# A hybrid mixer and MLP block on one core: gates by one Tanh, decays made earlier, a norm row by a product, and one product moved forward

## The chip, the core and the metric

The kernel runs on 1 core of a Trainium2 chip. TensorE (PE) multiplies, VectorE (DVE), ScalarE (ACT) and GpSimd (POOL) work element by element, and SyncE (SP) issues the DMAs, one after the other. The metric is device time in microseconds (us) of one execution; less is better. Three runs of the kernel before gave 1247.94, 1253.7 and 1256.1 us, with a median of 1253.7 us.

## What is computed

A sequence of 16 meta tokens and 1024 tokens, 1024 channels wide, goes through one block. All is float32. Cut to what matters here:

```python
u = rmsnorm(h, norm_mix)                        # y * g: a row of 1024 factors
a, q, k, v, r, lr, ga, gb = split(u @ w_in)
y_a = (multiscale_pool(a) @ w_pool_mix * pool_scale) @ w_pool_out
log_a = log_sigmoid(lr @ w_gate_up + b_gate) / 16        # decays, 256 wide
o = gla_chunked(q / 8, k, v, log_a)             # gated linear attention, chunks of 64
o = rmsnorm(o, gla_norm) * silu(r)              # silu(r) = r * sigmoid(r)
y_b = o @ w_gla_out
m = sigmoid(ga) * y_a + sigmoid(gb) * y_b
h = h + m @ w_out
h = h + square(relu(rmsnorm(h) @ w_ff1)) @ w_ff2
out = rmsnorm(h)[16:]
```

## The kernel before, in words

Data lie transposed: channels on the 128 partitions, 1024 tokens as two halves of 512 columns. PE has no exact float32 path at full rate here, so each float32 operand is split into a high part (`w1h`, `th`) by an ACT copy and a low part (`w1l`, `tl`) by a DVE subtraction, and `mm3` (L256) multiplies three times: high by high (L260), low by high and high by low (L261, L262). A product of one 512-row slice by 512 columns is 4 times 3, or 12 matmuls.

The order of PE's instructions is written out by hand. The other engines' orders are made by a scheduler from the program and its own estimates, and each engine, SP too, goes through its list strictly in order: an instruction that waits holds all behind it.

The stages are these.

- **Opening** (`start`, L391). SP loads `x` tile by tile; each tile is normalized (`layer_norm`, L227: a square with a sum on ACT, small steps on DVE, and a DVE product L234 with the norm row `gB`, a copy of the 1024 factors on all partitions that a 512 KB broadcast DMA makes, L414), turned by PE (L246), copied out (L202, L203, L249) and multiplied by the columns of `v` and `lr` (`v_tile`, L350). `warm` (L407) gives PE work on a blank tile.
- **Plain stage.** Blocks of 128 columns of `w_in` for `a` (L483) and `k` (L520), 8 by 24 matmuls and more each, with the pooling (`mix_block`, L495) between. `W1` is a ring of two weight blocks: when a block is done, the next but one is loaded and split (L75, L76). Their results leave through three PSUM banks `mm`.
- **Pairs** (`pairs_of_projections`, L688). The 22 blocks of q, r, gb and ga go two at a time through seven products instead of eight: P1, P2, P5, P6, P7, P4, P3. The differences of `x` that they need are made by `differences` (L529), the sums of weights by POOL (`sums_weights`, L641), and each is split by ACT (L609) and DVE (L610). `pairs_order` (L633) sets the order. P2 adds to the PSUM bank in which P1 stands, and P1 must be copied to `u2p` (L720) before it. The first pair's weights start in `first_pair` (L676). The tile of differences `xr` lies where `fs` and `u2p` lie afterwards, so the last one, made by `last_difference` (L551, split at L541 and L542), must be over before POOL writes `fs`.
- **What leaves the pairs.** `sigmoid` (L563) is the log of the sigmoid: Abs, Exp and Ln on ACT (L566, L567, L568) and one step on DVE (L569). `put_gate` (L583) stores it for ga and gb, and the Exp that ends it comes later, by `open_gate` (L967, instruction L970). `put_r` (L577) takes it on with an Exp (L579) and a DVE product (L580).
- **Inside a chunk** (`inside`, L842), four times, spread between the pairs' products. The decays `g` come from `log_decay` (L776: one product L779 into bank `gs`, four ACT steps, one DVE step) and an Exp (L855). Then levels 0 to 5 double the blocks: DVE and ACT grow the tiles `n` and `f` (L873, L875, L874), PE makes scores (L834) from them, and DVE writes those under a mask (L902). `meta_state` (L797) does the same for the 16 meta tokens.
- **Merge** (`gla`, L1107, and what follows). The attention across chunks (L1044 to L1105) runs between the products for y_a (`ya_block`, L976) and y_b (`yb_block`, L1004); the gates come back from DRAM, are opened by L970 and multiplied in (L996, L1025), and the sum is split again (L1029, L1030). Then `w_out`, the second norm, and the two MLP layers, which the change does not touch.

Of the kernel before, what the change touches and what calls it, by code (L numbers as in the profile page):

```python
# [103 lines left out]
def kernel(  # L104
# [50 lines left out]
    q_dram = dp.tile([2, 2, P, HALF], F32, name="q_dram")  # L155
    pm_dram = dp.tile([4, 2, P, HALF], F32, name="pm_dram")
# [234 lines left out]
    def start():  # L391
# [20 lines left out]
        warm(6)  # L412
        nc.sync.dma_start(ident, ident_in)
        nc.sync.dma_start(gB, bcast(norm_mix))  # L414
        for t in range(8):
# [9 lines left out]
            if t == 0:  # L425
                nc.sync.dma_start(S["lrraw"], w_in[:, C_LR : C_LR + 16].rearrange("(k p) c -> p k c", p=P))
                ask_vw(0)
                load(1)
                load(2)
                warm(10, P)  # L430
                load_vw(0)
                ask_vw(1)
# [29 lines left out]
    def quad(a):  # L462
        return a.rearrange("p (k c) -> p k c", k=4)

# [91 lines left out]
    for f, i in ((a_, 0), (a_, 1), (m_, 0), (a_, 2), (m_, 1), (a_, 3), (m_, 2), (k_, 0), (m_, 3)):  # L556
        f(i)
# [3 lines left out]
    step(one, lambda: S["last_difference"]())  # L561

    def sigmoid(b):  # L563

        t = nxt("t1")
        act.activation(t, b, ACT.Abs)  # L566
        act.activation(t, t, ACT.Exp, scale=-1.0)  # L567
        act.activation(t, t, ACT.Ln, bias=1.0)  # L568
        dve.scalar_tensor_tensor(t, b, 0.0, t, ALU.min, ALU.subtract)  # L569
# [7 lines left out]
    def put_r(h, half, b, o):  # L577
        t, o = sigmoid(b), o or nxt("c")
        act.activation(t, t, ACT.Exp)  # L579
        dve.scalar_tensor_tensor(o, b, gnorm[:, h : h + 1], t, ALU.mult, ALU.mult)  # L580
        nc.sync.dma_start(r_dram[h, half], o)

    def put_gate(dram):  # L583
        return lambda d, half, b, o: nc.sync.dma_start(dram[d, half], sigmoid(b))
# [48 lines left out]
    def pairs_order(n_pairs):  # L633
        yield from (("P1", 0), ("P2", 0), ("P5", 0))
        for i in range(1, n_pairs + 1):
            for p in ("P6", "P1", "P7", "P5", "P4", "P2", "P3"):
                n = i if p in ("P1", "P5", "P2") else i - 1
                if n < n_pairs:
                    yield p, n

    def sums_weights(order, n_pairs, load, eng):  # L641
# [5 lines left out]
        for p, i in order(n_pairs):  # L647
# [3 lines left out]
            else:  # L651
                a21, a22 = (w1raw[i, 1][:, k : k + 4] for k in (0, 4))
                s = quad(S["fs"][:, i % 2] if p != "P7" else S["s3"])
# [34 lines left out]
    def pairs_of_projections():  # L688
# [18 lines left out]
        for n, (p, i, (ah, al)) in enumerate(ahead(pair_weights(), 3)):  # L707
# [17 lines left out]
            elif p == "P7":  # L725
# [3 lines left out]
                put(d + 1, 1, c, c)  # L729
            elif p == "P4":  # L730
# [20 lines left out]
            if total - n == 3:  # L751
                raw.back()
                W1.shift = 1
                enqueue(rest)
                W1.top_up(1)
            yield

# [18 lines left out]
    def log_decay(lrT, p, n, dst, y, t):  # L776

        b = two("gs")[:, 0, :n]
        pe.matmul(b, wgu[:, p * P : (p + 1) * P], lrT, start=True, stop=True)  # L779
        act.activation(y, b, ACT.Identity, bias=bgate[:, p : p + 1])  # L780
# [755 lines left out]
```

## Time and profile before

The profiled execution took 1249.28 us, of which the program's span is 1247.4 us; 1.9 us lie around it.

| stretch of the span (us) | what runs | PE busy | DVE busy | ACT busy | DMA share |
|---|---|---|---|---|---|
| 0 to 26 | opening, up to the third tile | 22.16 | 15.31 | 18.00 | 0.83 |
| 26 to 152.6 | rest of the opening, plain stage | 126.39 | 64.62 | 56.57 | 0.28 |
| 152.6 to 408 | pairs, with the work inside chunks | 245.92 | 191.93 | 166.81 | 0.43 |
| 408 to 525 | across chunks, merge | 110.93 | 82.80 | 53.54 | 0.81 |
| 525 to 628 | `w_out`, second norm | 102.25 | 60.48 | 40.97 | 0.31 |
| 628 to 1247.4 | MLP, last norm | 605.99 | 450.91 | 299.45 | 0.50 |

How to read it: PE is busy nearly always, so what another engine does costs time only where PE waits for it. A row of the profile gives in brackets how long an engine stood idle before an instruction and which instruction ended that idle time. PE's matmuls overlap: a row's length is not the step from one to the next, which is read from their starts.

### The profile page before, as it was taken

The numbers are of one execution on the slowest core, as the hardware profiler recorded it, in microseconds if no ns is written. First come the engines' busy times: TensorE is split into PE (matmuls) and PEld (weight loads), VectorE is DVE, ScalarE is ACT, GpSimd is POOL, SyncE is SP. The second block draws the span as 40 slices with busy tenths as digits, with TensorE's granted clock in tenths as the row PEclk, the third lists the DMA queues.
The fourth block names the chain that finished last, engine by engine and source line by source line (L and its number), as shares of the span: only waits on it lengthen the run. The fifth ranks groups of instructions, "written<-read, shape, count | busy, mean of one in ns | idle before, by whom it ended". The sixth has DMA issues, their size and how long they took to land.

```text
span 1247.4 us, 18416 instructions
## 1 busy us (share of the span) xinstructions
PE 1213.6 (97%) x6807; PEld 997.3 (80%) x6807; DVE 866.0 (69%) x1421; ACT 635.3 (51%) x1119; POOL 72.2 (6%) x95
## 2 busy tenths in 40 slices
PE   8999999999999999999999999999999999999997
PEld 6999877777777778788778888888878788888776
DVE  5635548796877478844897676676664887887686
ACT  7623456767576434523655454554554444445454
POOL 0000042322321000000000000000000000000000
PEclk9999999999999999999999999999999999999999
DMA  8212342434347976941245444444579763333532
GB/s 259 81 39 85 94 127 76 136 97 141 80 134 229 327 264 200 311 138 51 101 125 161 145 157 150 157 152 144 168 241 368 274 214 102 102 93 93 169 91 86
DMA packets 153401, 192.23 MB, mean 154 GB/s; under 512 B 12096, under 2 KB 89168, under 8 KB 153312
## 3 DMA queue, kind: packets, MB, share of 16 engines
q1 hardware_dynamic: 153312, 191.06, 47.6%
q8 instruction: 53, 0.87, 0.3%
q14 instruction: 36, 0.29, 0.1%
HBM read 129.14 MB, written 61.88 MB: 153 GB/s over the span
## 4 chain that ended last, share of the span: by engine, by line
PE 76%; DVE 9%; DMA 8%; ACT 4%; issue 3%; SPq 1%; POOL 0%; DVEq 0%; ACTq 0%; POOLq 0%
PE b_o L261 7%; PE b_o L262 7%; PE b_o L260 7%; PE b_mm L262 6%; PE b_mm L260 6%; PE b_mm L261 6%; PE b_y L260 5%; PE b_y L261 5%; PE b_y L262 5%; PE b_sc L260 3%; PE b_sc L261 3%; PE b_z L260 3%; PE b_sc L262 3%; PE b_z L261 3%; PE b_z L262 3%
## 5 line engine op out<-in xcount | busy, mean ns | idle before, releaser
L609 ACT ACTIVATE w1h<-raw 128x512 fp32r<-128x512 f32 x106 | 66.0, 624 | 61.0 <-PE b_sc L261 19.5
L260 PE MATMUL b_sc<-th,w1h 128*128 128x512 f32 x216 | 86.4, 400 | 2.5 <-ACT u2p L720 1.8
L261 PE MATMUL b_sc<-tl,w1h 128*128 128x512 f32 x216 | 85.5, 396 | 0.0
L260 PE MATMUL b_z<-th,w1h 128*128 128x512 f32 x216 | 85.3, 395 | 0.2 <-DVE c L728 0.2
L262 PE MATMUL b_sc<-th,w1l 128*128 128x512 f32 x216 | 85.1, 394 | 0.0
L610 DVE TENSOR_TENSOR w1l<-raw,w1h 128x512 fp32r<-128x512 f32 x106 | 72.5, 684 | 18.0 <-ACT w1h L609 18.0
L261 PE MATMUL b_z<-tl,w1h 128*128 128x512 f32 x216 | 84.2, 390 | 0.4 <-DVE tl L1221 0.4
L262 PE MATMUL b_z<-th,w1l 128*128 128x512 f32 x216 | 84.1, 390 | 0.0
L260 PE MATMUL b_o<-w1h 128*128 128x512 f32 x192 | 75.6, 394 | 2.8 <-DVE h L1361 1.8
L609 ACT ACTIVATE w1h<-fs 128x512 fp32r<-128x512 f32 x81 | 50.9, 629 | 51.7 <-PE b_y L261 29.9
L261 PE MATMUL b_o<-w1l,w1h 128*128 128x512 f32 x192 | 75.6, 393 | 1.4 <-DVE w1l L610 1.4
L262 PE MATMUL b_o<-w1h,w1l 128*128 128x512 f32 x192 | 75.5, 393 | 0.1
L260 PE MATMUL b_mm<-th,w1h 128*128 128x512 f32 (+1 forms) x208 | 72.0, 346 | 0.9 <-DVE c L736 0.9
L610 DVE TENSOR_TENSOR w1l<-fs,w1h 128x512 fp32r<-128x512 f32 x81 | 56.8, 702 | 20.7 <-ACT w1h L609 20.6
L261 PE MATMUL b_mm<-tl,w1h 128*128 128x512 f32 (+1 forms) x208 | 71.1, 342 | 0.0
L262 PE MATMUL b_mm<-th,w1l 128*128 128x512 f32 (+1 forms) x208 | 71.0, 341 | 0.0
L609 ACT ACTIVATE w1h<-bt 128x512 fp32r<-128x512 f32 x45 | 28.3, 630 | 56.8 <-issue 33.0
L1409 DVE TENSOR_TENSOR bt<-w,w 128x512 f32<-128x512 f32 x80 | 54.7, 684 | 2.7 <-DMA w<-in_w_ff_dram 2.7
L260 PEld LDWEIGHTS b_sc<-th,w1h 128*128 128x128 f32 x216 | 40.9, 190 | 13.5 <-ACT u2p L720 2.2
L261 PE MATMUL b_o<-fxl,fxh 128*128 128x512 f32 x128 | 49.9, 390 | 0.7 <-DVE small L219 0.7
L260 PE MATMUL b_mm<-wo,th 128*128 128x512 f32 x128 | 50.4, 394 | 0.0
L262 PE MATMUL b_o<-fxh,fxl 128*128 128x512 f32 x128 | 49.9, 390 | 0.0
(375 smaller groups left out, 3345.7 us busy)
## 6 DMA issues: line engine op xcount, KB each, us to landing
hf_dram<-h SPq DMA_DIRECT2D x112, 256.0 KB, 2.1
raw<-hf_dram SPq DMA_DIRECT2D x112, 256.0 KB, 2.6
w<-in_w_ff_dram SPq DMA_DIRECT2D x64, 256.0 KB, 4.7
raw<-in_w_in_dram SPq DMA_DIRECT2D x22, 512.0 KB, 4.7
raw<-in_w_ff_dram SPq DMA_DIRECT2D x16, 512.0 KB, 4.2
rawx<-in_w_ff_dram SPq DMA_DIRECT2D x16, 512.0 KB, 4.3
rawp<-in_w_in_dram SPq DMA_DIRECT2D x10, 512.0 KB, 4.6
xs<-in_x_dram SPq DMA_DIRECT2D x8, 512.0 KB, 5.5
```

The costliest lines, as they stand in the source:

```text
L260: pe.matmul(ps, ah, bh, start=first and i == 0, stop=False, skip_group_check=more)
L261: pe.matmul(ps, ah, bl, start=False, stop=False, skip_group_check=more)
L262: pe.matmul(ps, al, bh, start=False, stop=last and i == n - 1, skip_group_check=more)
L609: act.activation(hi, a, ACT.Copy)
L610: dve.tensor_tensor(lo, a, f32(hi), ALU.subtract)
L1409: dve.tensor_tensor(bt, w, S["w2"][q[3:]][:, i], ALU.add if q[2] == "+" else ALU.subtract)
```

## The change

- **Gates.** `sigmoid` becomes `half_tanh`: one ACT Tanh of half the argument. A sigmoid is half of one plus this Tanh, so `ya_block` and `yb_block` add 1 in the DVE product that was there, and the factor 0.5 goes into the copy and the subtraction that split the sum. `open_gate` and its 32 Exps are gone.
- **r.** `put_r` uses the Tanh, one ACT step that scales and adds (`gnorm` is halved beforehand), and a DVE product.
- **Decays.** `decays` makes all four half rows of decays in the plain stage, by the same steps in the bank `ms`, and stores them to `decay_dram`, 256 KB each; `inside` loads them. `meta_state`'s decays are made there too.
- **Table sets.** ACT's functions come in sets. Two more loads of a set stand in the program: one behind the decays, one behind the last gate.
- **First pair.** The order is P1, P4, P2, P5 instead of P1, P2, P5, with P4 left out later. Its result is kept in `g` by one ACT copy until P7. The weights of P4 and P2 are split before `last_difference`.
- **Norm row.** A 4 KB row is loaded, and two products with a row of ones copy it to all partitions, two DVE copies bring it to `gB`; four of six early `warm` matmuls stay. The loads for `v` are asked for earlier, `lr`'s behind them.

```diff
         load(0)
-        warm(6)
+        nc.sync.dma_start(um[:1], norm_mix[None, :])
         nc.sync.dma_start(ident, ident_in)
-        nc.sync.dma_start(gB, bcast(norm_mix))
+        ask_vw(0)
+        nc.sync.dma_start(S["lrraw"], w_in[:, C_LR : C_LR + 16].rearrange("(k p) c -> p k c", p=P))
+        pool.memset(xm[:1, :P], 1.0)
+        warm(2)
+        for c in halves():
+            b = bank("mm")
+            pe.matmul(b, xm[:1, :P], um[:1, c], start=True, stop=True)
+            dve.tensor_copy(gB[:, c], b)
+        warm(2)
...
+    def decays(p):
+        def fn():
+            for half, c in enumerate(halves()):
+                y = nxt("c")
+                log_decay(gB[:16, c], p, HALF, y, nxt("t1"))
+                act.activation(y, y, ACT.Exp, scale=1.0 / TAU)
+                nc.sync.dma_start(decay_dram[p, half], y)
+                yield 0.6
+            if p:
+                act.activation(gnorm, gnorm, ACT.Copy, scale=0.5)
+            log_decay(lrT_meta, p, META, metab[:, META_LOG[p]], metab[:, 4])
+            if p:
+                tc.keep_in_program_order(act.preload_act_table_set("exp_and_others"))
...
-    for f, i in ((a_, 0), (a_, 1), (m_, 0), (a_, 2), (m_, 1), (a_, 3), (m_, 2), (k_, 0), (m_, 3)):
+    for f, i in ((a_, 0), (d_, 0), (a_, 1), (d_, 1), (m_, 0), (a_, 2), (m_, 1), (a_, 3), (m_, 2), (k_, 0), (m_, 3)):
...
-    step(one, lambda: S["last_difference"]())
-
-    def sigmoid(b):
+    def after_keys():
+        S["first"] += [next(S["pw"]) for _ in range(2)]
+        S["last_difference"]()
+
+    step(one, after_keys)
+
+    def half_tanh(b):
 
         t = nxt("t1")
-        act.activation(t, b, ACT.Abs)
-        act.activation(t, t, ACT.Exp, scale=-1.0)
-        act.activation(t, t, ACT.Ln, bias=1.0)
-        dve.scalar_tensor_tensor(t, b, 0.0, t, ALU.min, ALU.subtract)
+        act.activation(t, b, ACT.Tanh, scale=0.5)
         return t
...
     def put_r(h, half, b, o):
-        t, o = sigmoid(b), o or nxt("c")
-        act.activation(t, t, ACT.Exp)
-        dve.scalar_tensor_tensor(o, b, gnorm[:, h : h + 1], t, ALU.mult, ALU.mult)
+        t, o, g = half_tanh(b), o or nxt("c"), gnorm[:, h : h + 1]
+        act.activation(t, t, ACT.Identity, scale=g, bias=g)
+        dve.tensor_tensor(o, b, t, ALU.mult)
         nc.sync.dma_start(r_dram[h, half], o)
...
-        yield from (("P1", 0), ("P2", 0), ("P5", 0))
+        yield from (("P1", 0), ("P4", 0), ("P2", 0), ("P5", 0))
...
-                if n < n_pairs:
+                if n < n_pairs and (p, n) != ("P4", 0):
...
+            elif p == "P4" and i == 0:
+                act.activation(S["g"], b, ACT.Copy)
...
+        tc.keep_in_program_order(act.preload_act_table_set("natural_log_exp_and_others"))
...
-        log_decay(gB[:16, half * HALF : (half + 1) * HALF], p, HALF, g, y, t)
-        act.activation(g, g, ACT.Exp, scale=1.0 / TAU)
+        nc.sync.dma_start(g, decay_dram[p, half])
         yield 4.5
...
-                    open_gate("a", d, h)
-                    open_gate("a", d + h, 1 - h)
...
-                    dve.tensor_tensor(o, b, o, ALU.mult)
+                    dve.scalar_tensor_tensor(o, o, 1.0, b, ALU.add, ALU.mult)
...
-                dve.tensor_tensor(gl, b, gl, ALU.mult)
+                dve.scalar_tensor_tensor(gl, gl, 1.0, b, ALU.add, ALU.mult)
                 dve.tensor_tensor(gl, gl, ml, ALU.add)
...
-                act.activation(th, gl, ACT.Copy)
-                dve.tensor_tensor(tl, gl, f32(th), ALU.subtract)
+                act.activation(th, gl, ACT.Copy, scale=0.5)
+                dve.scalar_tensor_tensor(tl, gl, 0.5, f32(th), ALU.mult, ALU.subtract)
```

How the orders move is seen in three places. A row gives the line, the operation, what is written and what is read; names have numbers where a tile exists more than once. The changed kernel's lines lie a few dozen lower.

First, ACT at the start of the pairs, before. `raw` is loaded weights, `th_143` the last difference, `fs` POOL's sum for P5, `b_sc` the bank of P1 and P2:

```order
L523 ACTIVATE c<-b_mm 128x264 x2
L609 ACTIVATE w1h<-raw_119 128x512
L541 ACTIVATE th_143<-xr 128x2048
L523 ACTIVATE c<-b_mm 128x512
L609 ACTIVATE w1h<-fs 128x512
L720 ACTIVATE u2p<-b_sc 128x512
```

And with the change:

```order
L558 ACTIVATE c<-b_mm 128x264 x2
L646 ACTIVATE w1h<-raw_124 128x512
L576 ACTIVATE th_144<-xr 128x2048
L646 ACTIVATE w1h<-raw_120 128x512
L558 ACTIVATE c<-b_mm 128x512
L646 ACTIVATE w1h<-fs 128x512
L757 ACTIVATE u2p<-b_sc 128x512
```

P4's weights (`raw_124`) now stand where P2's stood, P2's (`raw_120`) one place later, and the copy of P1 keeps its place behind the split of `fs`. On PE twelve matmuls of P4 stand between P1 and P2.

Second, ACT in the middle of the first `inside`, before. `t_1011` are the tiles of the sigmoid, `n_1669` carries the decays, `w1h` splits weights for the next products:

```order
L566 ACTIVATE t_1011<-b_sc 128x512
L567 ACTIVATE t_1011<-t_1011 128x512
L568 ACTIVATE t_1011<-t_1011 128x512
L609 ACTIVATE w1h<-fs 128x512
L579 ACTIVATE t_1011<-t_1011 128x512
L574 ACTIVATE c<-c 128x512
L780 ACTIVATE n_1669<-b_gs,small 128x512
L781 ACTIVATE n_1669<-n_1669 128x512
L782 ACTIVATE n_1669<-n_1669 128x512
L783 ACTIVATE n_1669<-n_1669 128x512
L609 ACTIVATE w1h<-rawp_1643 128x512
L855 ACTIVATE g<-g 128x512
```

With the change, from the same sigmoid to the same weights:

```order
L606 ACTIVATE t_1015<-b_sc 128x512
L616 ACTIVATE t_1015<-t_1015,small 128x512
L646 ACTIVATE w1h<-fs 128x512
L611 ACTIVATE c<-c 128x512
L905 ACTIVATE n_1729<-f 128x128x4
L646 ACTIVATE w1h<-rawp_1703 128x512
```

Twelve instructions have become six, and one of the six (`n_1729<-f`, level 0) stood behind all twelve.

Third, SP around the first `inside` with the change, where the decays are loaded. `rawp` and `raw` are weights of the pairs:

```order
L885 DMA gi<-q_dram 128x512
L99 DMA rawp_1699<-in_w_in_dram 128x8x128
L612 DMA q_dram<-c 128x512 x2
L886 DMA g<-decay_dram 128x512
L618 DMA r_dram<-c 128x512
L612 DMA q_dram<-c 128x512
L99 DMA rawp_1703<-in_w_in_dram 128x8x128
L886 DMA g<-decay_dram 128x512
L618 DMA r_dram<-c 128x512
L99 DMA raw_120<-in_w_in_dram 128x8x128
```

Before, no row of `g` stood there. The second load of `g`, for the second `inside`, stands among the first one's rows, so that it waits there for level 0 of the first; the third and fourth stand one `inside` ahead in the same way.

More of the change, by code (lines that the diff above doesn't have):

```diff
@@ L774, in pooled_part @@
             pooled_rows(3)
[L776 to L780, printed above, removed]
-        act.activation(t, y, ACT.Abs)
-        act.activation(t, t, ACT.Exp, scale=-1.0)
-        act.activation(t, t, ACT.Ln, bias=1.0)
-        dve.scalar_tensor_tensor(dst, y, 0.0, t, ALU.min, ALU.subtract)
     def blocks(a, m):
@@ L944 @@
     step(rest, gla_open)
[L946 removed]
+    wanted, have = [], {}
     def lend(*keys):
@@ L965, in ask @@
                 nc.sync.dma_start(o, dram[d, h])
-    def open_gate(*key):
-        if key in have and key not in opened:
-            opened.add(key)
-            act.activation(have[key][0], have[key][0], ACT.Exp)
     def take(*key):
```

39 lines of the change are left out of this document (24 added, 15 removed).

## The prediction, made before the changed kernel ran

> **What bounds the kernel now.** I read the page first, then the table by stretches, then the groups of PE's instructions stretch by stretch with the idle time before them, and last the rows around each long wait.
>
> ```profile
> PE 1213.6 (97%) x6807; PEld 997.3 (80%) x6807; DVE 866.0 (69%) x1421; ACT 635.3 (51%) x1119; POOL 72.2 (6%) x95
> 152.60:408.00 255.40, 245.92 (x1844) 189.91 (x1842) 191.93 (x315) 166.81 (x294) 70.83 (x88) 0.99 0.43 129
> 408.00:525.00 117.00, 110.93 (x819) 90.55 (x819) 82.80 (x142) 53.54 (x80) 0.00 (x0) 1.00 0.81 273
> ```
>
> PE is busy 97% of the span, and the second and third rows (length, then PE, weight loads, DVE, ACT, POOL, clock, DMA share, GB/s) cover what the change touches most: there PE idles 9.5 and 6.1 us. ACT and DVE are far from full. So the many ACT steps that go are worth only the PE waits that they cause. These are the groups behind which the idle time stands, in the pairs and then in the merge (busy time, mean ns, idle time, who ended it):
>
> ```profile
> L834 PE MATMUL b_gs<-n 64*64 64x64 f32 x768 | 17.1, 225 | 5.1 <-DVE gi L902 2.1 <-ACT t L567 1.3 <-ACT gi L858 1.2
> L260 PE MATMUL b_sc<-th,w1h 128*128 128x512 f32 x88 | 36.4, 413 | 1.8 <-ACT u2p L720 1.8
> L779 PE MATMUL b_gs<-gB,wgu 16*128 16x512 f32 x8 | 4.5, 640 | 1.5 <-DVE S L819 1.5
> L260 PE MATMUL b_mm<-th,w1h 128*128 128x512 f32 x64 | 26.0, 406 | 0.9 <-DVE c L736 0.9
> L260 PE MATMUL b_mm<-yg,w1h 128*128 128x512 f32 x57 | 22.6, 396 | 2.2 <-ACT w1h L75 1.1 <-DVE c L1025 0.6 <-DVE t L1025 0.5
> L262 PE MATMUL b_mm<-yg,w1l 128*128 128x512 f32 x57 | 22.4, 393 | 0.6 <-DVE w1l L76 0.6
> L1061 PE MATMUL b_m<-v,kt 64*64 64x128 f32 x64 | 2.2, 275 | 1.7 <-ACT kt L1056 1.6
> L1061 PE MATMUL b_sc<-v,kt 64*64 64x128 f32 x64 | 2.2, 272 | 1.5 <-DMA v<-v_dram 1.5
> ```
>
> These waits, 15.3 us together, with the clock that one of them costs, are all that can be won behind the opening.
>
> **First pair.** P2's first matmul waits for the copy of P1.
>
> ```profile
> 152.34 2.29 DVE L542 TENSOR_TENSOR tl<-xr,th 128x2048 fp32r<-128x2048 f32 x1 [1.11 <-ACT th L541]
> 154.77 1.42 POOL L645 TENSOR_TENSOR fs<-raw 128x256 f32<-128x256 f32 x2 [121.00 <-DVE tl L542]
> 156.22 0.63 ACT L609 ACTIVATE w1h<-fs 128x512 fp32r<-128x512 f32 x1 [2.76 <-POOL fs L645]
> 156.75 0.58 ACT L720 ACTIVATE u2p<-b_sc 128x512 f32<-128x512 f32 x1
> 157.39 0.50 PE L260 MATMUL b_sc<-th,w1h 128*128 128x512 f32 x1 [1.81 <-ACT u2p L720]
> 161.83 0.40 PE L260 MATMUL b_z<-th,w1h 128*128 128x512 f32 x1
> 164.58 0.39 PE L260 MATMUL b_y<-t0h,w1h 128*128 128x512 f32 x1
> 155.00:175.00 20.00, 18.19 (x73) 14.48 (x72) 8.04 (x11) 7.81 (x13) 10.51 (x15) 0.91 0.52 133
> ```
>
> The last difference ends on DVE at 154.63, POOL's sum at 156.19, its split at 156.85, the copy at 157.33; PE has been idle since 155.58. After the 1.81 us of idling P2 takes 161.83 - 157.39 = 4.44 us, P5 behind it 164.58 - 161.83 = 2.75; the granted clock in that stretch is 0.91. So the wait costs 1.81 + 1.69 = 3.5 us. With P4 between, twelve matmuls of 2.75 us run from some 155.4 to 158.2, past the copy's end. P4's weights are split at the place of P2's, well ahead; P2's split comes one DVE step (0.69) later, which could push the copy to 158.0 at most. What is late next would be P5's low part, wanted at 160.9; it ended at 156.88 + 1.22 = 158.1. The new copy of P4's result is one ACT step in a gap. I take 3.5; at the least 1.8, if the clock sinks anyhow.
>
> [...]
>
> **Gates, r and decays: what they free.**
>
> ```profile
> L568 ACT ACTIVATE t<-t 128x512 f32<-128x512 f32 x40 | 25.1, 628 | 0.9
> L780 ACT ACTIVATE n<-b_gs,small 128x512 f32<-128x512 f32 x4 | 2.7, 679 | 0.1
> L569 DVE SCALAR_TENSOR_TENSOR t<-c,t 128x512 f32<-128x512 f32 x30 | 21.7, 724 | 18.0 <-ACT t L568 18.0
> ```
>
> Forty results go through the sigmoid. Each loses two of three ACT steps (80 by 0.63 = 50 us) and its DVE step (40 by 0.72 = 29 us); a Tanh is not in the trace, and I price it as the Ln of the same shape, 0.63. Decays take 4 by 0.68 and 16 by 0.63 = 13 us of ACT out of this stretch. So ACT falls from 167 to about 104 us of 255, DVE from 192 to about 160. None of this is PE time.
>
> The two waits of L779 are for DVE's copy of the meta state out of the bank `gs`. The decay's product no longer uses that bank, and products that need none of it follow: 1.5 us gone. The product itself moves: the same eight matmuls in the plain stage, cost unchanged.
>
> The score waits, 5.1 us, stand behind full queues. Two of them, 1.27 and 1.14 us, come at the end of a dense stretch of DVE:
>
> ```profile
> 204.89 0.69 DVE L569 SCALAR_TENSOR_TENSOR t<-c,t 128x512 f32<-128x512 f32 x1 [1.42 <-ACT t L568]
> 208.62 0.68 DVE L569 SCALAR_TENSOR_TENSOR t<-b_sc,t 128x512 f32<-128x512 f32 x1
> 212.89 1.23 DVE L569 SCALAR_TENSOR_TENSOR t<-c,t 128x512 f32<-128x512 f32 x1
> 211.94 0.71 PE L834 MATMUL b_gs<-n 64*64 64x64 f32 x32 [1.27 <-ACT t L567]
> 216.77 0.71 PE L834 MATMUL b_gs<-n 64*64 64x64 f32 x32 [1.14 <-DVE gi L902]
> 353.37 0.84 DVE L862 TENSOR_TENSOR n<-gi,g 128x512 f32<-128x512 f32 x1 [2.76 <-DMA gi<-q_dram]
> ```
>
> The three L569 rows, 2.6 us, go, as much as PE waited. The 1.2 us behind ACT's L858, and what follows them, come from the last row: the fourth `inside` starts late on its load of q. In the new order no 512 KB load of the second norm row stands before it, and its decays were loaded an `inside` earlier, so most of this goes too. I take 4.0 of 5.1, with 1.0 and 5.1 as ends.
>
> **Merge.** The opening of gates on ACT waits for a DMA, and the next ACT step behind it.
>
> ```profile
> 455.02 0.63 ACT L970 ACTIVATE o<-o 128x512 f32<-128x512 f32 x1 [2.77 <-DMA o<-gb_dram]
> 455.56 0.58 ACT L1056 ACTIVATE kt<-b_ms 128x512 f32<-128x512 f32 x1
> ```
>
> `kt` was ready to be copied out before; without L970 the 1.6 us before L1061 nearly vanish. The 1.5 us for `v` stay: its load stands on SP behind loads into the gates' tiles as before. Of the 2.8 us around L1025, L75 and L76 I take 0.7, one Exp's length out of the chain from load to sum; DVE still waits for the loads. The 0.9 behind L736 is the time to empty the last bank and stays. Taken 2.1; ends 0 and 4.4. DVE's product becomes a scalar-tensor-tensor, which takes 0.68 in the rows of L569: no loss.
>
> **Opening.** 512 KB less are loaded, but PE waits on DVE there:
>
> ```profile
> 7.06 1.28 DVE L234 SCALAR_TENSOR_TENSOR us<-xs,small,gB 128x1024 f32<-128x1024 f32 x1
> 10.04 1.23 DVE L342 TENSOR_TENSOR vw<-raw,vw 128x1024 fp32r<-128x1024 f32 x1 [1.49 <-ACT vw L341]
> 13.70 0.39 PE L261 MATMUL b_mm<-vw,th 128*128 128x272 f32 x1 [0.18 <-DVE vw L342]
> L260 PE MATMUL b_mm<-vw,th 128*128 128x272 f32 x24 | 7.2, 299 | 1.2 <-ACT th L202 1.2
> ```
>
> The two copies out of PSUM come ahead of L234 in DVE's list; at 0.68 each, the price of the L569 row that reads the bank `b_sc`, L234 starts at 8.4 instead of 7.06. The 1.49 us of waiting for weights at 10.04 go in return. From there DVE's list adds up as before: 8.4 + 1.28 + 2 by 1.23 + 2 by 0.68 (the low parts of the tile) gives 13.5, and `lr`'s small low part is now last, for the point that was 13.70. What the smaller load saves goes to DVE. Later tiles come earlier, but ACT, 18 of the first 26 us busy, has to take them, so I take 0, with 2.2 (the waits of tiles two and three) and -1.0 as ends.
>
> **Plain stage.** ACT gets two parcels there, of 2 by 0.68, 8 by 0.63 and the small meta steps, 7.3 us, the second with a table load.
>
> ```profile
> 0.73 1.28 ACT L392 ACT_TABLE_LOAD   x1 [0.73 <-PEq L1525]
> 90.52 1.06 ACT L75 ACTIVATE w1h<-raw 128x1024 fp32r<-128x1024 f32 x1 [4.83 <-PE b_mm L261]
> 101.84 1.06 ACT L75 ACTIVATE w1h<-raw 128x1024 fp32r<-128x1024 f32 x1 [4.86 <-PE b_mm L261]
> ```
>
> A block lasts 11.3 us, and its weights' split (1.06, then 1.23 on DVE) may start 9.0 us late before PE notices. The second parcel is 7.3 + 1.28 = 8.6. I take 0, with -2.0 as the end.
>
> [...]
>
> **Sum.** 3.5 + 1.5 + 4.0 + 2.1 = 11.1 us. The profiled execution's 1249.28 becomes 1238.2. It lies 4.4 below the median shown, so for a median I expect 1253.7 - 11.1 = 1242.6. Ends: 1.8 + 1.5 + 1.0 + 0 - 1.0 - 2.0 = 1.3, and 3.5 + 1.5 + 5.1 + 4.4 + 2.2 = 16.7.
>
> **Rivals.** (1) *All waits go.* With ACT at 40% nothing is late, in the opening too: 16.7 us, 1237.0. For it: DVE and ACT rows cause nearly all waits. Against: DMA in the merge is as busy as before. (2) *DVE still sets the scores.* ACT's relief is idle, DVE at 63% keeps bursts as dense as at 210; only the first pair, L779 and 1 us of the rest go: 6.0 us, 1247.7. Against it stand the three L569 rows. (3) *Slower: SP is held by the decays.* A load of `g` waits for level 0 of the running `inside`, and the pairs' weights stand behind it. If they come late, PE waits for a load from its issue on, 4.7 us, and its clock sinks as at the first pair, 1.7: three times 6.4 is 19.2 us, and 1242.6 + 19.2 = 1261.8. A product takes 2.75, a pair of seven 19.3 us; a load lands in 4.7 us, so it decides when SP is held above 14 us.
>
> ```profile
> 201.62 14.71 SPq L581 DMA_DIRECT2D r_dram<-c  x4
> L877 DVE TENSOR_TENSOR ends<-g x4: 415/420/427, 193.3 to 358.5; 128x256 f32<-128x256 f32 x4
> raw<-in_w_in_dram SPq DMA_DIRECT2D x22, 512.0 KB, 4.7
> ```
>
> Against it: SP spends 14.7 us on four stores of r already, with no wait of PE for weights, and the last reader of `g` (L877) is through at 193.7, before that. (4) *It doesn't do what it says*: Tanh and Ln mix and ACT reloads tables. The order shows two loads more, so hardly.
>
> **How the numbers follow.** Chances: forecast 0.56, all go 0.16, DVE sets 0.19, slower 0.07, not done 0.02. About 1%, 12.5 us, is what a measurement of this kernel can tell from no change. The forecast's own spread (8 to 15 us) lies above that in 0.25 of its 0.56; with rival 1 that is 0.41 for faster. Rival 3 gives 0.02 beyond 1% on the other side, were the waits longer; the rest, 0.57, is within. The range goes from 1233 (16.7 below the profiled run) to 1250 (a gain of 4).
>
> **What would show it.** Right: no gap before P2 and a clock near 1.0 from 155 to 175; no wait of L779's successor; under 1.5 us before scores; no wait for `kt`; ACT near 104 us in the pairs; the third tile's product within 1 us of 25.7. Wrong: a PE wait for L75's weights in the plain stage, a wait for `g` or for pair weights behind it, or score waits that stay with ACT idle.

## The result, and the profile after

The changed kernel takes 1241.7 us (median of five runs, 1240.37 to 1242.05) where the kernel before takes 1252.67 us on the same chip (five runs, 1247.94 to 1256.1). The ratio is 0.9915, with a 95% interval of 0.9890 to 0.9939: 11.0 us less. That is clear of no change, but whether it reaches 1% (12.5 us) can't be told. In a later set the same pair gave 1242.33 and 1251.56 us, a ratio of 0.9922 (0.9895 to 0.9949). The forecast was 1242.6 us.

The time came out as predicted; the profile did not. The profiled execution after took 1242.05 us, 7.2 less than the 1249.28 of the profile before, where the sum asked for 11.1. A second profile of each kernel gave 1243.93 and 1249.59, a difference of 5.7. Two executions below ran slow, one of 1344.36 us (old gates) and one of 1725.6 us at a granted clock of 0.656 (the profiled one of v ahead of the gates, which was therefore profiled again), and no number is read from either.

The first fence is the row of busy times from the page after, the second the table by stretches: the pairs, from P1 to the first product of y_a, and from there to `w_out` (length, PE, weight loads, DVE, ACT, POOL, clock, DMA share, GB/s).

```profile
PE 1213.4 (98%) x6807; PEld 997.9 (80%) x6807; DVE 841.8 (68%) x1383; ACT 575.2 (46%) x1011; POOL 75.1 (6%) x96
```

```profile
158.30:401.70 243.40, 238.96 (x1831) 188.58 (x1830) 161.71 (x253) 112.12 (x187) 73.63 (x88) 0.99 0.46 141
401.70:512.00 110.30, 104.70 (x793) 85.93 (x794) 77.13 (x134) 33.15 (x47) 0.00 (x0) 1.00 0.81 267
```

ACT lost 60 us in all and DVE 24, and PE's idle time in the pairs fell from 9.5 us to 243.40 - 238.96 = 4.4. PE's groups show what is left of it, first in the whole span, then in the second stretch (busy time, mean ns, idle time before them and who ended it):

```profile
L867 PE MATMUL b_gs<-n 64*64 64x64 f32 x768 | 17.0, 225 | 3.6 <-DVE gi L933 3.6
L261 PE MATMUL b_sc<-th,w1h 128*128 128x512 f32 x216 | 85.6, 396 | 0.5 <-ACT u2p L1355 0.5
```

```profile
L261 PE MATMUL b_mm<-yg,w1h 128*128 128x512 f32 x56 | 22.2, 396 | 1.6 <-ACT w1h L75 1.5
L1083 PE MATMUL b_m<-v,kt 64*64 64x128 f32 x64 | 2.2, 275 | 3.1 <-DMA v<-v_dram 3.1
L1083 PE MATMUL b_sc<-v,kt 64*64 64x128 f32 x64 | 2.2, 272 | 0.3 <-DMA v<-v_dram 0.3
```

The score waits fell from 5.1 to 3.6 us only, and all of them now stand behind DVE's masked write. P2 (the second row, together with the MLP's product) no longer waits: the starts of P1, P2 and P5 follow without a gap.

```profile
158.32 0.40 PE L261 MATMUL b_sc<-th,w1h 128*128 128x512 f32 x1
163.85 0.40 PE L261 MATMUL b_sc<-th,w1h 128*128 128x512 f32 x1
166.65 0.40 PE L261 MATMUL b_z<-th,w1h 128*128 128x512 f32 x1
```

The wait for `kt` is gone, and the one for `v` grew from 1.5 to 3.4. The larger of the score waits has a tail. Here is PE's timeline behind it, and the row of the table by stretches:

```profile
211.56 0.71 PE L867 MATMUL b_gs<-n 64*64 64x64 f32 x32 [2.81 <-DVE gi L933]
212.20 0.79 PE L261 MATMUL b_y<-t0h,w1h 128*128 128x512 f32 x1
212.79 0.63 PE L262 MATMUL b_y<-t0l,w1h 128*128 128x512 f32 x1
```

```profile
210.00:215.00 5.00, 3.44 (x39) 2.82 (x40) 4.97 (x10) 2.91 (x6) 1.43 (x2) 0.72 0.28 105
215.00:220.00 5.00, 5.00 (x50) 3.88 (x49) 5.00 (x9) 2.51 (x5) 1.87 (x2) 0.94 0.15 56
```

Matmuls that take 0.39 us at full rate take 0.63; the clock column reads 0.72 and 0.94, so 5 times 0.28 and 5 times 0.06, 1.7 us, are lost behind the wait. The clock that sank behind P2 before now sinks here.

The starts of PE's rows give the stages of every trace used below (us; *decays* says whether they are made in the plain stage):

| trace | first v tile | first block of a | a to P1 | P1 to y_a | y_a to `w_out` | profiled run |
|---|---|---|---|---|---|---|
| before | 13.15 | 79.19 | 73.43 | 255.30 | 111.01 | 1249.28 |
| before, again | 12.90 | 82.10 | 73.43 | 254.66 | 110.31 | 1249.59 |
| after | 16.74 | 80.37 | 77.95 (decays) | 243.41 | 110.22 | 1242.05 |
| after, again | 16.08 | 79.75 | 77.95 (decays) | 245.09 | 110.74 | 1243.93 |
| old opening | 13.30 | 81.60 | 77.95 (decays) | 243.94 | 110.10 | 1244.74 |
| old first pair | 13.01 | 80.51 | 77.95 (decays) | 240.18 | 111.25 | 1240.16 |
| old gates | 13.07 | 77.22 | 77.95 (decays) | 246.91 | 112.67 | 1246.55 |
| P4 in u3p | 13.08 | 77.36 | 77.97 (decays) | 238.75 | 110.45 | 1234.89 |
| P4 in u3p, v behind four gates | 12.99 | 77.43 | 77.97 (decays) | 238.68 | 108.46 | 1231.93 |
| the same, old opening | 12.98 | 81.00 | 77.95 (decays) | 238.63 | 106.93 | 1234.34 |
| P4 in u3p, old gates | 13.04 | 77.43 | 77.97 (decays) | 246.74 | 113.34 | 1247.19 |
| before with decays | 12.77 | 80.02 | 77.97 (decays) | 247.71 | 114.69 | 1250.77 |
| v ahead of gates, again | 12.95 | 77.67 | 77.95 (decays) | 243.64 | 111.36 | 1240.8 |

The plain stage takes 4.5 us more wherever the decays are made there, and no row of PE waits in it. So 4.5 of the 11.9 us that the pairs lose are only moved.

### The profile page after: what moved, and what is told of

Same layout as the page of the kernel before. It is cut to its first block, busy times and chain, and to the rows that moved or that the text cites. A ratio compares the mean times of both kernels' runs of the same rounds, so it can differ in the third digit from the quotient of the medians.

```text
span 1240.2 us, 18304 instructions
## 1 busy us (share of the span) xinstructions
PE 1213.4 (98%) x6807; PEld 997.9 (80%) x6807; DVE 841.8 (68%) x1383; ACT 575.2 (46%) x1011; POOL 75.1 (6%) x96
## 4 chain that ended last, share of the span: by engine, by line
PE 87%; DVE 6%; DMA 3%; issue 2%; ACT 1%; SPq 0%; POOL 0%; DVEq 0%; ACTq 0%; POOLq 0%
PE b_o L262 7%; PE b_o L263 7%; PE b_o L261 7%; PE b_mm L263 7%; PE b_mm L261 7%; PE b_mm L262 7%; PE b_y L261 6%; PE b_y L262 6%; PE b_y L263 6%; PE b_sc L261 4%; PE b_sc L262 4%; PE b_z L261 4%; PE b_sc L263 4%; PE b_z L262 4%; PE b_z L263 4%
## 5 line engine op out<-in xcount | busy, mean ns | idle before, releaser
L263 PE MATMUL b_mm<-wo,tl 128*128 128x512 f32 x128 | 49.9, 390 | 0.0
```

The costliest lines, as they stand in the source:

```text
L263: pe.matmul(ps, al, bh, start=False, stop=last and i == n - 1, skip_group_check=more)
```

## The experiments

### Each part undone

**The old opening alone.** The changed kernel, with the broadcast load, six `warm` matmuls ahead and the loads in the old order:

```diff
-        nc.sync.dma_start(um[:1], norm_mix[None, :])
+        warm(6)
         nc.sync.dma_start(ident, ident_in)
...
-        for c in halves():
-            b = bank("mm")
-            pe.matmul(b, xm[:1, :P], um[:1, c], start=True, stop=True)
-            dve.tensor_copy(gB[:, c], b)
-        warm(2)
+        nc.sync.dma_start(gB, bcast(norm_mix))
```

> The changed kernel with the old opening alone: the 512 KB broadcast of the norm row, six warm matmuls ahead, the loads in the old order; all else as changed. If the one-row product and the new order cost time in the opening, as the two traces suggest (first product of a v tile 3.6 us later, first block of a 1.2 us later), the first v tile starts near 13.2 us again and the time is 1.2 us less, 1240.5. If what the opening loses is made up elsewhere anyway, 1241.7. If the broadcast is what makes the kernel before vary by 8 us from run to run, this kernel varies likewise and its median rises by up to 4 us, to 1245.7.

Measured: 1243.03 us (1239.9 to 1244.74, before 1251.55), a ratio of 0.9923 (0.9906 to 0.9939), the same as the change's. The first v tile is at 13.30 again, but the first block of a comes at 81.60, later than in the changed kernel. So the first theory falls: the old opening as a whole is not faster. That the late v tile costs nothing does not follow. By the table, five traces with the new opening, an early v tile and no sinking clock ahead of it start `a` at 77.2 to 77.7, the change's two late ones at 79.8 and 80.4, so lateness costs 2 to 3 us there. The runs spread by 4.8 us.

**The old first pair alone.** P1, P2, P5, and P4 after P7:

```diff
-        yield from (("P1", 0), ("P4", 0), ("P2", 0), ("P5", 0))
+        yield from (("P1", 0), ("P2", 0), ("P5", 0))
...
-        S["first"] += [next(S["pw"]) for _ in range(2)]
         S["last_difference"]()
...
-                if i == 0:
-                    c = nxt("c")
-                    dve.tensor_tensor(c, S["g"], u3, ALU.add)
-                    put(d + 1, 0, c, c)
-            elif p == "P4" and i == 0:
-                act.activation(S["g"], b, ACT.Copy)
```

> The changed kernel with the old order of the first pair (P1, P2, P5 and P4 after P7; the weights of P2 split after the last difference). If that step is worth what the prediction priced, 1.8 us of waiting and 1.7 us of a lower clock, the gap before P2 is back, the granted clock from 160 to 180 is near 0.91, and the time is 1241.7 + 3.5 = 1245.2. If the clock sank for another reason, only the gap is back: 1243.5. If the time won there is lost again at a later wait, 1241.7.

Measured: 1238.06 us (1236.15 to 1240.16, before 1251.55), ratio 0.9892 (0.9876 to 0.9907). None of the three came: undoing the step that the prediction priced at 3.5 us made the kernel some 3 us faster by the ratios, whose intervals overlap a little. Its timeline, its table by stretches and its groups say why not, and then why:

```profile
163.24 0.50 PE L261 MATMUL b_sc<-th,w1h 128*128 128x512 f32 x1 [1.81 <-ACT u2p L756]
```

```profile
160.00:165.00 5.00, 3.19 (x15) 2.27 (x14) 1.70 (x2) 1.11 (x2) 3.75 (x6) 1.00 0.82 225
```

```profile
L860 PE MATMUL b_gs<-n 64*64 64x64 f32 x768 | 17.0, 225 | 0.0
```

The gap before P2 is back to the hundredth (the clock stayed at 1.00 this time), but not one score waits. So P4 in second place costs something at the scores, 40 us behind it. The tile rows of `g` in the changed kernel show a candidate:

```profile
L886 SPq DMA_DIRECT2D g<-decay_dram x2: 405/420/436, 185.6 to 197.5; - x2
L772 ACT ACTIVATE g<-b_y x1: 581/581/581, 166.8 to 166.8; 128x512 f32<-128x512 f32 x1
L769 DVE TENSOR_TENSOR c<-g,u3p x1: 677/677/677, 182.0 to 182.0; 128x512 f32<-128x512 f32 x1
```

```profile
190.92 0.82 DVE L893 TENSOR_TENSOR n<-gi,g 128x512 f32<-128x512 f32 x1 [4.53 <-DMA g<-decay_dram]
```

`g` is the tile of the decays. From 166.8 to 182.7 it holds P4's result for P7, so the first decays are not asked for before 185.6, and DVE stands 4.53 us idle until 190.92 before it can begin the first `inside`.

**The old gates alone.** Log of the sigmoid, its Exps in the merge, no other table set:

```diff
-        act.activation(t, b, ACT.Tanh, scale=0.5)
+        act.activation(t, b, ACT.Abs)
+        act.activation(t, t, ACT.Exp, scale=-1.0)
+        act.activation(t, t, ACT.Ln, bias=1.0)
+        dve.scalar_tensor_tensor(t, b, 0.0, t, ALU.min, ALU.subtract)
```

> The changed kernel with the old log of the sigmoid for gates and r, its Exps in the merge and no other load of a table set; decays, first pair and norm row stay as changed. If the Tanh frees scores and merge as predicted (4.0 less what L779 had, and 2.1), the time is 6.1 us more, 1247.8. If, as the trace of the change reads, only 1.5 us of the score waits went and the merge gave back as much as it won, 1.5 to 2 us more, 1243.5. If ACT's relief is worth nothing, 1241.7.

Measured: 1248.3 us (1245.57 to 1250.28, before 1251.55), ratio 0.9973 (0.9960 to 0.9985). That is 6 to 7 us above the change, the first of the three. The pairs take 246.91 against 243.41 and y_a to `w_out` 112.67 against 110.22, 3.5 and 2.5 us. The clock sinks once in each trace for 1.7 us, in the pairs of the change and in the merge here; without these dips the differences would be 5.2 and 0.8.

**The decays alone**, on the kernel before: `decays` in the plain stage, `inside` loading them, no Tanh, no change of tables.

```diff
+        nc.sync.dma_start(g, decay_dram[p, half])
-        log_decay(gB[:16, half * HALF : (half + 1) * HALF], p, HALF, g, y, t)
-        act.activation(g, g, ACT.Exp, scale=1.0 / TAU)
```

> The kernel before with the decays made in the plain stage and stored, as in the change, and nothing else of it; the gates keep the log of the sigmoid. The prediction's terms that hang on the decays are L779's 1.5 us and some 1.2 us of the score waits behind the fourth inside's late load; the products themselves only move (4.1 us more before P1, as much less behind it). So 1251.6 - 2.7 = 1248.9, no PE wait in the plain stage, none at the meta state. If the decays' ACT steps in the plain stage or the loads of g cost as much as they save, 1251.6.

Measured: 1248.73 us (1245.13 to 1251.95, before 1249.6), ratio 0.9989 (0.9975 to 1.0003): not to be told from nothing. The trace has both halves. From P1 to y_a 255.30 - 247.71 - 4.5 = 3.1 us are won, near the 2.7 expected, and the meta state's products wait no more. But y_a to `w_out` takes 114.69: PE waits 3.24 us for `v` at 419.95, and its clock sinks behind it for twice 1.7 us. So in this trace the decays' gain is spent there.

### What holds the scores

**P4's result in another tile.** The changed kernel, with two words exchanged; the second half of `u3p` is free until the second pair's P7:

```diff
-                    dve.tensor_tensor(c, S["g"], u3, ALU.add)
+                    dve.tensor_tensor(c, S["u3p"][:, 1], u3, ALU.add)
...
-                act.activation(S["g"], b, ACT.Copy)
+                act.activation(S["u3p"][:, 1], b, ACT.Copy)
```

> The changed kernel with P4 second, but its result kept in the second half of u3p instead of in g; nothing else differs. Theory: what the first pair wins is lost because g is also the tile of the first decays; they can be loaded only after P7, DVE starts the first inside some 4.5 us late and the scores at 205 and 211 wait 3.6 us, behind which the clock sinks once for about 1.7 us. Then the decays are loaded ahead of the pairs, these waits go, the gap before P2 stays away, and the time is 1241.7 - 5.3 = 1236.4, some 1.7 us under the kernel with the old first pair (1238.06). Rival: the two DVE steps that P4's result takes behind P7, or the order that the scheduler makes with them, delay the scores wherever the result is kept; then the waits of 0.8 and 2.8 us stay and the time is 1241.7.

Measured: 1237.58 us (1234.89 to 1238.56, before 1249.6), ratio 0.9900 (0.9880 to 0.9921). By the ratios that is some 2 to 3 us less than the change, less than the 5.3 of the theory, and the intervals overlap; the trace has to carry it. P1 to y_a takes 238.75 us, 4.7 to 6.3 less than in the change's two traces. The row of DVE's timeline, the group of the scores and the row of the pairs:

```profile
174.47 0.83 DVE L893 TENSOR_TENSOR n<-gi,g 128x512 f32<-128x512 f32 x1 [3.33 <-DMA gi<-q_dram]
```

```profile
L867 PE MATMUL b_gs<-n 64*64 64x64 f32 x768 | 17.0, 225 | 0.0
```

```profile
155.30:394.10 238.80, 237.59 (x1832) 187.36 (x1830) 160.07 (x247) 113.07 (x187) 71.41 (x88) 1.00 0.47 143
```

The first `inside` begins 16.4 us earlier (13.5 counted from P1, which is itself 3.0 earlier), no score waits, the clock stays at 1.00, and PE idles 1.2 us in the pairs instead of 4.4. P4 is second as before, and its two DVE steps are there; in the program only the tile differs, and what the scheduler reorders follows from it. So the hold of `g` is shown to be the cause of these waits, and the rival falls. Against the old first pair (0.9892) the two times cannot be told apart; the trace gives P4's second place 240.18 - 238.75 = 1.4 us in an execution whose clock did not sink at P2.

**The old gates without that hold.** The same kernel with the edit of the old gates:

```diff
-                act.activation(S["g"], b, ACT.Copy)
+                act.activation(S["u3p"][:, 1], b, ACT.Copy)
...
-        act.activation(t, b, ACT.Tanh, scale=0.5)
+        act.activation(t, b, ACT.Abs)
```

> The kernel with P4's result in u3p (1237.6), with the old log of the sigmoid for gates and r and its Exps in the merge. There the tile g no longer holds the first inside, so what is left of the score waits is the gates' alone. By the prediction's terms (4.0 of the score waits less 1.2 that the decays took, and 2.1 in the merge) the time is 4.9 us more, 1242.5; the scores near 211 and 216 wait for the last step of the log of the sigmoid again, in sum 2 to 4 us between P1 and y_a. If the hold of g was the whole cause of the waits that stayed, and ACT's relief is worth little, no wait before scores exceeds 0.5 us and the time is 1237.6 to 1239.

Measured: 1248.09 us (1244.07 to 1251.26, before 1251.56), ratio 0.9971 (0.9952 to 0.9991). By the ratios the Tanh is worth 0.0071 of 1250, 8.9 us (the intervals allow 4 to 14), more than either theory gave; by the traces it is 8.0 us in the pairs and 2.9 behind them. Its groups and its row of the pairs:

```profile
L865 PE MATMUL b_gs<-n 64*64 64x64 f32 x768 | 17.1, 225 | 3.6 <-DVE gi L931 1.1 <-ACT t L603 0.9 <-ACT gi L887 0.8
L261 PE MATMUL b_sc<-th,w1h 128*128 128x512 f32 x216 | 85.7, 397 | 3.1 <-DVE t L605 1.7 <-DVE c L616 0.9 <-ACT u2p L1362 0.5
```

```profile
155.40:402.10 246.70, 239.02 (x1831) 187.07 (x1829) 185.47 (x285) 153.87 (x266) 75.84 (x88) 1.00 0.46 137
```

PE idles 7.7 us, 3.6 before scores and the rest mostly before P1 products that wait for DVE's step behind the sigmoid. This kernel and the old gates with P4 in `g` take the same (0.9971 and 0.9973). So each of two things is enough to make the scores late, the log of the sigmoid or the held tile; with the tile still held the Tanh wins 3.5 us of the 8.0 in the pairs, and with the old gates kept, freeing the tile wins next to nothing (246.91 to 246.74).

### What holds v

The v loads stand on SP behind loads into gates' tiles. SP's queue in the changed kernel:

```profile
402.73 1.46 SPq L996 DMA_DIRECT2D c<-ga_dram  x3
406.31 2.02 SPq L996 DMA_DIRECT2D t<-ga_dram  x3
408.38 2.72 SPq L968 DMA_DIRECT2D v<-v_dram  x4
```

**v ahead of all gates and chunk tiles:**

```diff
+        for half in range(2):
+            for p in range(2):
+                t = slice(4 * half, 4 * half + 4)
+                nc.sync.dma_start(S["v"][:, p, t], v_dram[p, t].rearrange("t p c -> p t c"))
         for p in range(2):
             fetch(p, 0)
         ask()
```

> The changed kernel with the four loads of v issued ahead of the loads of gates and of the chunk tiles. If PE's 3.1 and 0.3 us before the products of v and kt are owed to the place of these loads on SP alone, both go and the time is 1241.7 - 3.4 = 1238.3. If the loads wait for the space that the pairs leave, or if the loads of gates that now come behind them make PE wait in their place, 1241.7.

Measured: 1242.99 to 1244.76 us in three runs, ratio 0.9938 (0.9922 to 0.9955), the change's own time within what can be told. Its second profile:

> The changed kernel with the four loads of v ahead of the loads of gates and chunk tiles, profiled again (the first profile ran at 0.66 of the clock, so its waits say nothing). Its median was 2.7 us above the change. Theory: the wait before the products of v and kt is gone, but the chunk tiles or gates that now load behind them make PE wait between 402 and 430 us, for more than the 3.4 us saved. Rival: nothing new waits there, the stretch from y_a to w_out is some 3 us shorter than the change's 110.2, and the 2.7 us come from elsewhere or from chance.

Measured: 1240.8 us in one run. SP's queue and the row of PE that waits:

```profile
400.24 1.04 SPq L965 DMA_DIRECT2D v<-v_dram  x2
401.32 0.74 SPq L973 DMA_DIRECT2D gi<-gi_dram  x1
402.17 1.47 SPq L996 DMA_DIRECT2D c<-ga_dram  x3
```

```profile
410.05 0.66 PE L1077 MATMUL b_sc<-ident,gi 128*128 128x128 f32 x4 [3.29 <-DMA gi<-gi_dram]
```

`v` is there in time, and PE waits 3.29 us for the chunk tile that `v` was put ahead of. A wait was exchanged for another, as the theory had it, but for as much and not for more.

**v between the gates**, on the kernel with P4 in `u3p`: chunk tiles first, four gates, v, then the other gates.

```diff
+        wanted[:] = later[:4]
+        ask()
+        for half in range(2):
+            for p in range(2):
+                t = slice(4 * half, 4 * half + 4)
+                nc.sync.dma_start(S["v"][:, p, t], v_dram[p, t].rearrange("t p c -> p t c"))
+        wanted.extend(later[4:])
         ask()
```

> As the kernel with P4's result in u3p, and the four loads of v issued behind the first four loads of gates and ahead of the other ones. If PE's wait before the products of v and kt (1.5 to 3.4 us in the traces so far) is owed to the place on SP, it goes and the time is 1236.4 - 2.5 = 1233.9. If, as in the kernel with v ahead of all gates (2.7 us slower than the change), the loads of gates that come later make PE wait in their place, the trace shows such a wait in the products of y_a between 402 and 430, and the time is 1236.4 or up to 2.7 us more, 1239.1.

Measured: 1234.65 us (1231.93 to 1236.95, before 1249.6), ratio 0.9877 (0.9854 to 0.9900), 2.9 us under the kernel without it, with overlapping intervals. SP's row and the group of PE:

```profile
396.61 2.23 SPq L969 DMA_DIRECT2D v<-v_dram  x4
```

```profile
L1086 PE MATMUL b_m<-v,kt 64*64 64x128 f32 x64 | 2.2, 275 | 0.0
```

The wait (1.71 and 0.72 us in the kernel without it) is gone and next to nothing took its place: y_a to `w_out` takes 108.46 us against 110.45. This kernel is clearly faster than the one before; against the change and against P4 in `u3p` alone the intervals of the ratios overlap, and the traces carry the difference.

### Executions and openings

> The kernel before, profiled once more. Theory: the waits of PE stand at the same places in every execution, and behind a wait of 1.7 us or more the granted clock sinks in some executions and not in others, at 1.7 us each; how many of them do sets most of the spread of 9 us between runs, together with the opening. Then this trace shows the same waits within 0.5 us each, dips at other places than 156 and 928, and a first block of a within 77 to 82 us. Rival: the spread comes from DMA, and waits for transfers differ by several us between the two traces while the clock's dips stand at the same places.

Measured: 1249.59 us. From the pairs on, the waits of the kernel before stand at the same places, most of them to the hundredth (1.81 before P2, 1.27 and 1.14 before scores, 1.76 before the second layer), and three of the merge differ by 0.7 to 1.0 (the one for `kt` is down from 1.64 to 0.67). The dip behind P2 is there again (in 160 to 165), the one at 928 is not, and there is a new one in the opening, which ends 2.9 us later:

```profile
160.00:165.00 5.00, 4.70 (x14) 3.70 (x15) 2.31 (x3) 1.68 (x4) 2.90 (x4) 0.66 0.65 180
...
28.00:32.00 4.00, 4.00 (x21) 4.00 (x22) 1.88 (x4) 3.02 (x6) 0.00 (x0) 0.63 0.84 257
```

So the theory holds for the waits, for the opening (`a` at 82.1, at the edge of the 77 to 82 expected) and for one of two dips. No transfer's wait in the merge differs by several us, but both profiled executions of this kernel are about as fast, so what makes its slower runs of 1253 to 1258 us is not seen.

> The changed kernel itself, profiled and timed once more, beside the others of this set. Theory: in its first profile the early matmuls ran at the slow rate until 17 us by the chance of that execution, and the waits from 205 to 212 belong to the kernel. Then this trace has its first v tile near 13.0 and its first block of a near 77.4 (as three of the four other traces with this opening), the waits of 0.8 and 2.8 us stand at the same scores, and the stretch from P1 to the first product of y_a takes 243.4 us or, where the clock does not sink behind 2.8 us, 241.7. Rival: the one-row products keep the clock low in this kernel; then the first v tile is at 16.7 again.

Measured: 1242.33 us (1240.15 to 1243.93). The rival's sign came: the first v tile is at 16.08 again. But the same code runs early in other traces, as shown next, so it does not keep the clock low each time. The score waits are 1.21 and 2.82 us, and the clock sinks twice as long behind them, which is the 1.7 us that its pairs take more.

The opening of the change was in eight traces. Here are its first rows of PE, of the change and of the kernel with P4 in `u3p`, whose opening has the same code:

```profile
1.46 3.78 PE L410 MATMUL b_ms<-xr 128*128 128x512 f32 x4 [1.46 <-POOL xr L406]
5.17 3.78 PE L421 MATMUL b_mm<-um,xm 1*128 1x512 f32 x4
8.88 3.78 PE L410 MATMUL b_ms<-xr 128*128 128x512 f32 x4
12.45 1.06 PE L247 MATMUL b_sc<-ident,us 128*128 128x128 f32 x4
```

```profile
1.46 3.78 PE L410 MATMUL b_ms<-xr 128*128 128x512 f32 x4 [1.46 <-POOL xr L406]
5.17 2.22 PE L421 MATMUL b_mm<-um,xm 1*128 1x512 f32 x4
7.32 1.98 PE L410 MATMUL b_ms<-xr 128*128 128x512 f32 x4
9.60 0.66 PE L247 MATMUL b_sc<-ident,us 128*128 128x128 f32 x4 [0.30 <-DVE us L235]
```

In the second the rate of PE doubles within the one-row products, before 6 us; in the first the transposes at 12.45 still take 1.06 us instead of 0.66, and the rate doubles at 14. Six traces go the second way, the change's two the first (12.9 in its second trace).

**The best kernel with the old opening** (the edit of the first experiment on it):

```diff
+        warm(6)
...
+        nc.sync.dma_start(gB, bcast(norm_mix))
```

> The kernel with P4's result in u3p and the loads of v behind four gates (1234.65), with the old opening: 512 KB broadcast, six warm matmuls, old order of loads. The first block of a started at 79.2, 82.1, 80.0 and 81.6 us in four traces with the old opening, 80.7 on the mean, and at 80.4, 80.5, 77.2, 77.4 and 77.4 in five with the new one, 78.6. If that difference is the opening's, this kernel takes 2.1 us more, 1236.8 (3.4 where the new opening is undisturbed, 1238.0). If the five and four traces differ by chance, 1234.65.

Measured: 1236.17 us (1234.34 to 1238.56, before 1251.56), ratio 0.9872 (0.9847 to 0.9898). The first block of a is at 81.00, 3.6 us later than with the new opening, but the ratio is that of the new opening (0.9877). Of the 3.6 us, 1.5 come back between y_a and `w_out` (106.93 against 108.46), where the clock sinks once with the new opening (behind the wait for L75's weights) and not with the old one; that is a chance of the execution as far as these traces tell. The traces favour the new opening; the times do not tell.

## Why the prediction came out, point by point

- **First pair, 3.5.** P1 to P5 takes 166.65 - 158.32 = 8.33 us with P4's 2.75 in it, where it took 9.21 without: 3.6 won at this place, with no gap before P2. The step that failed stands in the same paragraph: "The new copy of P4's result is one ACT step in a gap." Its length was looked at, and not the tile that it fills. What the runs showed in its place is that the copy held `g`, the tile of the first decays, so that their load came 4.53 us too late for DVE and 4.7 us of the pairs were lost at the scores. The prediction had the warning at hand, since rival 3 asked who holds a load of `g`, but it asked that of the running `inside` alone.
- **L779, 1.5.** Right: no such wait in any trace with the decays moved.
- **Score waits, 4.0 of 5.1.** Mis-sized: 1.5 went, and 1.7 of clock came behind the largest of those left. The reason was right for its own part. Without the hold all 5.1 go, and with the old gates 3.6 come back. Score waits that stay with ACT idle were named as the sign of a wrong step. Rival 2 (DVE still sets the scores) described what was seen, though not its cause: DVE was late because it began late, not because it was full.
- **Merge, 2.1.** Mis-sized: 0.8 in the first pair of traces; 0.4 lost in the second, where the clock sank for 1.7 behind the wait for `v`. The 1.6 of `kt` and the 1.1 around L1025 went. "The 1.5 us for `v` stay" failed: they became 3.4, because `v` now stands behind six gate loads with all four of its own. Moving it between them takes it away.
- **Opening, 0.** In its range: 1.2 us later in the first pair of traces, 2.4 earlier in the second. The copies made L234 later: worked out was 8.4, and the trace with P4 in `u3p` has 8.26. In the change it began at 9.71, because the one-row products ran at half their rate; that PE would stay at that rate until 13 or 14 was not foreseen, and it cost the 2 to 3 us named above. The third tile's product came at 26.9, 1.2 behind the mark instead of within 1.
- **Plain stage, 0.** Right: no wait for L75's weights, and 4.5 us added for the 4.8 that the products took in the pairs. Moving them was nearly free.
- **ACT near 104 us in the pairs:** 112.1; the Tanh rows are as short as priced (0.63, and 0.58 out of PSUM), the rest of the estimate was low.

So at their places the terms give 3.6 + 1.5 + 1.5 - 1.7 + 0.8 - 1.2 = 4.5 of the 7.2 us between the two profiles; 0.3 more is the decays' matmuls, which by their starts took 4.8 us of PE in the pairs and made the plain stage 4.5 longer. Of the last 2.4, 1.9 lie in the steps from one matmul of the pairs' products to the next: away from the sinking clock such a step is mostly 0.23 us, but 0.29 to 0.39 next to a wait or where scores or decays come between. There are 77 of these long steps before and 62 after, and what they take beyond 0.23 sums to 8.3 and 6.4 us. The median fell by 11.0 all the same, because the profiled execution of the kernel before lay 3.4 under its median and that of the change 0.4 over its own. The prediction took over the first of these distances (4.4 to the median then shown) and gave the gain 3.9 too high; the number was met by luck, because the two errors offset. Its range has a slip too: the low end, 1233, is counted from the profiled run and the forecast from the median, from which it would be 1237. What makes the kernel before slower in most of its other runs no trace shows.

## What to carry to other kernels

When a result is parked in a tile for a few steps, look up every later writer of that tile: here the saving of one wait held a load back, and 4.7 us were lost 40 us further on. When an engine is relieved and the waits stay, ask when its work could begin, not only how full it is, since two causes that are each enough hide one another's price. A load that is moved ahead of another only exchanges waits until both are in front of what is not needed yet.

## What the runs showed of the hardware

The clock's dips have one size. By the records of the granted clock there are 23 in the 13 traces, up to PE's last matmul. Each halves PE's rate for 3.41 us, which loses 1.7 us (4 times 0.28 and 0.15 in the stretches from 156 and 160 in the trace before, 4 times 0.43 in that from 212 after), or for twice as long where a second follows at once. They come behind waits of 1.5 us and more, once behind two of 1.0 and 0.9 us close together. The same wait sinks the clock in some executions and not in others: P2's 1.81 us in three of four, the 1.76 before the second layer in six of 13, the 2.8 before the score in four of four.

In eight traces with two dips or more, the dips stand whole numbers of 3.413 us apart, within 0.1 us. In the traces of before and of the change the records of the granted clock begin at 7.56 and 14.21 us, and the dips start at 157.75, 929.16 and 212.18: 44, 270 and 58 times 3.413 us later. Counted in steps of this length, PE idled 1.81, 1.76 and 2.79 us in the steps right ahead of these three dips. In before no dip followed any other step, and the most idle of these held 1.49 us. In the change none followed 1.77 us (before the second layer), nor the 3.11 for `v`, which lie as 1.86 and 1.25 in two steps. So near 1.8 us it went both ways, and what decides there is not shown. In the old first pair the dips start, by stretches of 4 us, at 22.1 and 411.2, 114 times 3.413 us apart; P2's 1.81 us lie there as 0.6 and 1.2 in two steps, and no dip followed.

The start of PE's full rate varies as well. It is at 7.56 us in the trace before and at 14.21 in the change's first trace (where the records of the clock begin), at 12.9 in the change's second and before 6 in the kernel with P4 in `u3p` (by PE's rows). The last three openings have the same code. Why it came late in the change's two traces is not shown: no run with products of full height in place of the one-row ones and all else equal was made.

The kernel before has a product of PE that is not split: L779, 512 columns in float32. It takes 1.05 us from its start to the next matmul's (183.90 to 184.95), where a matmul of split operands with 512 columns is followed by the next after 0.23, three of them after 0.68. How exact either is no trace tells.
